# The first stage of a hybrid SSD and retention layer: tokens first in the load queue, and two k-tiles of weights for three token blocks while two blocks arrive

## The chip, the cores and the metric

The kernel runs on one NeuronCore of one Trainium2 chip. The metric is the time of one execution on the device in microseconds. The engines are TensorE (PE, its weight loads PEld), VectorE (DVE), ScalarE (ACT), GpSimd (POOL), and SyncE (SP), which issues nearly all loads.

## What is computed

One layer of a bidirectional mixer for 640 tokens: 128 context tokens (token block 0, with modulation from `c_ctx`) and 512 latent tokens (blocks 1 to 4, with modulation from `c`). The reference, cut to what matters here:

```python
mod = jax.nn.silu(cond) @ w_mod + b_mod              # (1024) @ (1024, 3072)
shift, scale, gate = jnp.split(mod, 3, axis=-1)
h = _rms(x, norm_pre_w) * (1 + scale) + shift        # (tokens, 1024)
u = h @ w_in                                         # then split: z, xbc, dt, q, k, v, g
# SSD scan on xbc and dt, retention on q, k, v, both directions, each gated
out = mix @ w_out
y = x + gate * _rms(out, norm_post_w)
```

`_rms(x, w)` divides each token by the root of its mean square and multiplies by `w`. The first stage of the kernel makes h, all 640 tokens by 1024 channels, and with it the first 512 columns of u (256 columns of v and 256 of g).

## The kernel before, in words

Tokens come in five blocks t = 0..4 of 128 rows, channels in eight k-tiles kt = 0..7 of 128. Every product is made of three matmuls on split operands: a float32 value is a rounded high half and a low half, and hi x hi, hi x lo and lo x hi are added in PSUM.

The first stage is written as a list of steps, START (line 44): a letter and a k-tile or token block. The loop at line 352 issues each step's instructions in that order; a scheduler may let neighbours pass each other on an engine, but each engine then works strictly in its order. The steps:

- M kt (`load_wm`, line 245): SP loads the shift and scale columns of w_mod for k-tile kt, 128 x 2048, 1 MB, into one of three buffers (wm). W kt (`load_w0`, 250): the first 512 columns of w_in for k-tile kt, 256 KB, one of three buffers (raw). L t (`load_x`, 255): token block t, 512 KB, five buffers (x).
- A kt (`mod_a`, 290): modulation of k-tile kt on TensorE, 8 matmuls of 32 x 256 in 16 passes (mod<-wm,silc), and a copy on VectorE (ms). B kt (`mod_b`, 312): two small products that turn the row into columns (mod<-idt,ms), then two VectorE instructions that give shift and scale per channel (ash).
- N t (`norm_x`, 273): square and sum of a token block on ScalarE (hl<-x, L274), the power -0.5 on POOL (rs), and the scaling of its first 128 channels on VectorE. R t (`rest_x`, 337): the scaling of the other 896 channels, on VectorE after h of k-tile 0.
- H kt:ts (`h_tile`, 320): for token blocks ts, transposes on TensorE into PSUM (tr<-idt,x), on ScalarE scale and shift (h<-tr,ash, one instruction for block 0 and one for the others), on VectorE the split into halves (hh, hl).
- S kt (`split0`, 302): ScalarE rounds raw to w0h, VectorE makes w0l. G kt:ts (`gemm0`, 341): for each token block three matmuls of 128 x 512 (acc<-w0h,hh; acc<-w0l,hh; acc<-w0h,hl) into that block's PSUM bank.
- Z n (`warm`, 285): 4n matmuls of 128 x 128 on a tile of zeros, whose results nobody reads. F n: loads of the next stage's weights. C: two tables (cst, rope).

All loads of START stand in one queue of SP, in the order of the steps. When G7 is done, the next stage starts with the product gt (`gemm_tok`) on h of all k-tiles; the rest of the kernel follows an order of slots and does not depend on START.

```python
    for op in START.split():
        k = int(op[1])
        if op[0] == "H":
            h_tile(k, [int(t) for t in op[3:]])
        elif op[0] == "G":
            for t in op[3:]:
                gemm0(k, int(t))
```

Of the kernel before, what the change touches and what calls it, by code (L numbers as in the profile page):

```python
# [25 lines left out]
Z0, XS0, B0, C0, DT0, Q0, K0, V0, G0 = 0, 1024, 2048, 2560, 3072, 3104, 3616, 4128, 5152  # L26
# [15 lines left out]


START = """
M0 Z2 W0 L0 L1 L2 L3 L4 M1 W1 M2 N0 S0 A0 B0 H0:0 G0:0 R0 Z4 N1 H0:1 N2 N3 R1 H0:2 G0:1 H0:3 W2 M3
N4 W4 R2 R3 H0:4 R4 A1 S2 G0:4 W3 G0:3 B1 S1 S3 G0:2 H1:4 A2 W5 H1:0123 M4 B2 M5 H2:012 H2:3 H2:4
G1:01 G1:2 G2:12 G2:3 A3 G1:34 G2:4 B3 H3:0123 S4 G2:0 A4 H3:4 M6 G3:012 B4 H4:0123 H4:4 A5 G3:34 C0
M7 W7 S5 W6 B5 H5:0123 G4:012 A6 G4:34 F2 S6 B6 H5:4 H6:0123 H6:4 G5:012 A7 G5:34 F2 B7 S7 H7:0123
G6:34 G6:012 H7:4 F2 G7:012 G7:34
"""  # L50


# [53 lines left out]
def body(ctx, tc, io):  # L106
# [23 lines left out]
    def tt(out, a, b, op, eng=vec):  # L130
        return eng.tensor_tensor(out=out, in0=a, in1=b, op=op)  # L131
# [50 lines left out]
    def feed(ahead_load=4, ahead_split=2):  # L182
        while state["ld"] < min(len(want), state["use"] + ahead_load):
            pieces[state["ld"]] = load_split(state["ld"])
            state["ld"] += 1
        while state["sp"] < min(state["ld"], state["use"] + ahead_split):
            pieces[state["sp"]][2]()
            state["sp"] += 1
# [84 lines left out]
    def norm_x(t):  # L273
        act.activation(junk, xs_t[t], AF.Square, scale=1.0 / 32, accum_out=ss[:, t:t + 1])  # L274
        tt(rs[:, t:t + 1], ss[:, t:t + 1], mhalf[:, 0:1], ALU.pow, eng=pool)
        scale_x(t, slice(0, P), vec)

    def scale_x(t, q, eng):
        eng.tensor_scalar(xs_t[t][:, q], xs_t[t][:, q], rs[:, t:t + 1], None, op0=ALU.mult)
# [5 lines left out]
    def warm(n):  # L285
        wps = bank("warm")
        for _ in range(4 * n):
            mm(wps[:, 0:P], wz, wz, True, True)
# [31 lines left out]
    def h_tile(kt, ts):  # L320
        ash = ash_t[kt]
        h32 = st_.tile([P, 512], F32, tag="h32", name="h32", bufs=3)[:, 0:len(ts) * P]
        tr = bank("tr")
        for n, t in enumerate(ts):
            pe.transpose(tr[:, n * P:(n + 1) * P], xs_t[t][:, kt * P:(kt + 1) * P], ident)
        for c, u in ((0, [t for t in ts if t == 0]), (1, [t for t in ts if t])):
            if u:
                q = slice((u[0] - ts[0]) * P, (u[-1] + 1 - ts[0]) * P)
                act.activation(h32[:, q], tr[:, q], AF.Identity,
                               bias=ash[:, c:c + 1], scale=ash[:, 2 + c:3 + c])  # L330
        q = slice(ts[0] * P, (ts[-1] + 1) * P)
        vec.tensor_copy(hh[:, kt, q], h32)
        r = tt(hl[:, kt, q], h32, hh[:, kt, q].bitcast(F32), ALU.subtract)
        if kt == 0:
            h_last[ts[0]] = getattr(r, "ins", r)
# [5 lines left out]
    def gemm0(kt, t):  # L341
        wh, wl = w0[kt]
        s = slice(t * P, (t + 1) * P)
        mm(acc[t], hh[:, kt, s], wh, kt == 0, False)
        mm(acc[t], hh[:, kt, s], wl, False, False)
        mm(acc[t], hl[:, kt, s], wh, False, kt == KT - 1)

    acc = [pg.tile([P, 512], F32, tag="g", name="acc0") for _ in range(5)]
    steps = {
        "M": load_wm, "W": load_w0, "L": load_x, "A": mod_a, "S": split0, "B": mod_b, "N": norm_x, "R": rest_x,  # L350
    }
    for op in START.split():
        k = int(op[1])
        if op[0] == "H":
            h_tile(k, [int(t) for t in op[3:]])
        elif op[0] == "G":
            for t in op[3:]:
                gemm0(k, int(t))
        elif op[0] == "Z":
            warm(k)  # L360
        elif op[0] == "F":
            feed(k, 0)
        elif op[0] == "C":
            sp.dma_start(out=cst, in_=io["cst"])
            sp.dma_start(out=rope, in_=io["rope"])
        else:
            steps[op[0]](k)


    R = {}  # L370
# [90 lines left out]
    S = {}  # L461
# [482 lines left out]
    op = tc.alloc_tile_pool(name="op", bufs=1, side="right")  # L944
# [207 lines left out]
```

## Time and profile before

| | |
|---|---|
| median of 3 runs | 607.87 us (607.24 to 608.06) |
| profiled execution | 606.02 us, span 604.0 us, mean granted clock 0.993 |
| TensorE busy | 582.3 us (96% of the span) |
| VectorE / ScalarE / POOL busy | 418.1 (69%) / 337.4 (56%) / 31.3 us (5%) |
| DMA | 87.44 MB, 145 GB/s mean over the span |
| chain of waits that ended last | TensorE 65%, VectorE 13%, ScalarE 9%, DMA 6% |

The span runs from the first to the last instruction; the execution's own time has 2.0 us around it. A busy share is an average over stages with different limits, so the first stage is read from its own stretch. In a timeline row, "xN" is how many instructions were merged, and the bracket is the idle time before the row with what ended it.

### The profile page before, as it was taken

The page shows a single profiled execution, that of the slowest core. Times are in us where ns is not written, and L with a number is a line of the kernel's source. Part 1 is how long each engine was busy: PE and PEld are TensorE (multiplying, and loading weights), DVE is VectorE, ACT ScalarE, POOL GpSimd, SP SyncE. Part 2 cuts the span into 40 slices and gives each one's busy share as a digit, 9 for nine tenths or more (in the row PEclk, how much of TensorE's full clock was granted, in tenths as well). Part 3 has the DMA queues.
Part 4 walks back from the last instruction along what each step waited for, and adds up shares of the span by engine and source line. Part 5 has one row for each costly group of instructions (what it writes and reads, how often), then busy time and mean ns, then how long its engine had stood idle before and what let it go on. Part 6 is the DMA issues. An engine that isn't in the chain of part 4 may idle for free.

```text
span 604.0 us, 10966 instructions
## 1 busy us (share of the span) xinstructions
PE 582.3 (96%) x3833; PEld 521.5 (86%) x3833; DVE 418.1 (69%) x942; ACT 337.4 (56%) x934; POOL 31.3 (5%) x112
## 2 busy tenths in 40 slices
PE   5899998999999999999999999999999999999995
PEld 3577998978999998889999888999999777788895
DVE  3657498855698866668897746798867866743665
ACT  5436255665667764465766646566755857262421
POOL 1000001200000010000011000000110000000010
PEclk9899999999999999999999999999999999999998
DMA  8694231553335633232554223354537777384033
GB/s 348 229 362 161 63 105 48 162 146 109 99 97 159 185 91 86 80 122 70 189 172 112 76 69 105 102 163 131 160 96 223 209 266 221 116 272 120 18 109 135
DMA packets 47638, 87.44 MB, mean 145 GB/s; under 512 B 5792, under 2 KB 18656, under 8 KB 46048
## 3 DMA queue, kind: packets, MB, share of 16 engines
q1 hardware_dynamic: 47296, 86.57, 45.2%
q8 instruction: 30, 0.49, 0.3%
q14 instruction: 24, 0.20, 0.1%
q10 hardware_dynamic: 288, 0.18, 0.1%
HBM read 75.03 MB, written 9.60 MB: 140 GB/s over the span
## 4 chain that ended last, share of the span: by engine, by line
PE 65%; DVE 13%; ACT 9%; DMA 6%; issue 5%; POOL 2%; SPq 0%; POOLq 0%; DVEq 0%; ACTq 0%
PE gw L123 24%; PE gc L123 11%; PE gt L123 9%; PE acc L123 5%; PE go L123 4%; DMA cf<-cumd 3%; PE ss L123 2%; PE mod L123 2%; DVE wlo L131 2%; DVE SC L128 2%; PE sfb L123 1%; PE ry L123 1%; POOL sm L131 1%; DVE yc L128 1%; ACT jk L733 1%
## 5 line engine op out<-in xcount | busy, mean ns | idle before, releaser
L131 DVE TENSOR_TENSOR wlo<-raw,whi 128x512 fp32r<-128x512 f32 (+1 forms) x120 | 82.2, 690 | 49.2 <-ACT whi L174 48.3
L174 ACT CAST whi<-raw 128x512 fp32r<-128x512 f32 (+1 forms) x120 | 73.6, 619 | 76.3 <-PE gw L123 46.1
L123 PE MATMUL gc<-hh,whi 128*128 128x320 f32 x384 | 96.7, 331 | 0.0
L123 PE MATMUL gc<-hl,whi 128*128 128x320 f32 x384 | 88.3, 310 | 0.0
L123 PE MATMUL gc<-hh,wlo 128*128 128x320 f32 x384 | 87.6, 309 | 0.0
L123 PEld LDWEIGHTS gc<-hh,whi 128*128 128x128 f32 x384 | 63.9, 189 | 1.1
L123 PEld LDWEIGHTS gc<-hl,whi 128*128 128x128 f32 x384 | 64.3, 188 | 0.1
L123 PEld LDWEIGHTS gc<-hh,wlo 128*128 128x128 f32 x384 | 64.1, 188 | 0.0
L123 PE MATMUL gw<-whi,hh 128*128 128x512 f32 x120 | 50.6, 421 | 0.8 <-ACT u L484 0.8
L123 PE MATMUL gw<-whi,hl 128*128 128x512 f32 x120 | 47.0, 392 | 0.0
L123 PE MATMUL gw<-wlo,hh 128*128 128x512 f32 x120 | 46.8, 390 | 0.0
L123 PE MATMUL gt<-whi,hh 128*128 128x256 f32 (+1 forms) x160 | 46.3, 289 | 0.0
L123 PE MATMUL gt<-wlo,hh 128*128 128x256 f32 (+1 forms) x160 | 45.7, 286 | 0.0
L123 PE MATMUL gt<-whi,hl 128*128 128x256 f32 (+1 forms) x160 | 45.7, 286 | 0.0
L862 ACT ACTIVATE m<-gu,dt 128x128 f32<-128x128 f32 x80 | 31.3, 391 | 16.5 <-DVE gu L131 14.6
L834 ACT ACTIVATE cf<-cf,dmc 128x128 f32<-128x128 f32 x80 | 26.5, 393 | 18.4 <-DMA cf<-cumd 18.4
L131 DVE TENSOR_TENSOR m<-m,cf 128x512 f32<-128x512 f32 x40 | 27.5, 689 | 8.8 <-ACT cf L863 8.2
L123 PE MATMUL gw<-whi,mrh 128*128 128x512 f32 x80 | 32.3, 404 | 0.0
L123 PE MATMUL gw<-wlo,mrh 128*128 128x512 f32 x80 | 31.2, 391 | 0.0
L123 PEld LDWEIGHTS gt<-whi,hh 128*128 128x128 f32 x160 | 30.5, 190 | 0.7 <-issue 0.5
L863 ACT ACTIVATE cf<-gu,dt 128x128 f32<-128x128 f32 x80 | 31.0, 387 | 0.0
L123 PE MATMUL gw<-whi,mrl 128*128 128x512 f32 x80 | 30.9, 391 | 0.0
(232 smaller groups left out, 1327.8 us busy)
## 6 DMA issues: line engine op xcount, KB each, us to landing
raw<-ws SPq DMA_DIRECT2D x116, 256.0 KB, 2.8
cf<-cumd SPq DMA_DIRECT2D x20, 512.0 KB, 4.2
wm<-wm SPq DMA_DIRECT2D x8, 1024.0 KB, 8.2
mraw<-mixd SPq DMA_DIRECT2D x16, 320.0 KB, 3.4
ef<-ecumd SPq DMA_DIRECT2D x32, 128.0 KB, 3.3
wg<-wg SPq DMA_DIRECT2D x4, 1024.0 KB, 5.9
x<-x SPq DMA_DIRECT2D x5, 512.0 KB, 7.3
mixd<-rmix SPq DMA_DIRECT2D x20, 128.0 KB, 2.7
```

Of the source, the lines that this page charges most:

```text
L123: r = pe.matmul(out, lhsT=a, rhs=b, start=start, stop=stop)
L128: eng.scalar_tensor_tensor(out=out, in0=in0, scalar=s, in1=in1, op0=op0, op1=op1)
L131: return eng.tensor_tensor(out=out, in0=a, in1=b, op=op)
L174: act.copy(hi, raw)
L733: act.activation(jk, yc[:, h], AF.Square, scale=P ** -0.5, accum_out=sm[:, 2 + h:3 + h])
L834: act.activation(cf[:, e, 1, q], cf[:, e, 1, q], AF.Identity, bias=dmc[:, c, h:h + 1])
L862: act.activation(m[:, e, q], gu[:, 0], AF.Copy, scale=dt[:, c, h:h + 1])
L863: act.activation(cf[:, e, 1, q], gu[:, 1], AF.Copy, scale=dt[:, c, 16 + h:17 + h])
```

## The change

The list START is written anew, and the scaling of the first 128 channels becomes a step of its own, Q, which N included before. Tokens stand first in the load queue and are mixed with the weights of k-tiles 0 and 1; k-tile 0 and 1 are multiplied for blocks 0 to 2 before blocks 3 and 4 follow; from then on a line of the list does the modulation of k-tile kt, the products of k-tile kt-2, and the transposes of kt-1 between these. Z18 stands at the start, further Z steps between the first steps; all of Z come to 132 matmuls instead of 24.

```diff
 START = """
-M0 Z2 W0 L0 L1 L2 L3 L4 M1 W1 M2 N0 S0 A0 B0 H0:0 G0:0 R0 Z4 N1 H0:1 N2 N3 R1 H0:2 G0:1 H0:3 W2 M3
-N4 W4 R2 R3 H0:4 R4 A1 S2 G0:4 W3 G0:3 B1 S1 S3 G0:2 H1:4 A2 W5 H1:0123 M4 B2 M5 H2:012 H2:3 H2:4
-G1:01 G1:2 G2:12 G2:3 A3 G1:34 G2:4 B3 H3:0123 S4 G2:0 A4 H3:4 M6 G3:012 B4 H4:0123 H4:4 A5 G3:34 C0
-M7 W7 S5 W6 B5 H5:0123 G4:012 A6 G4:34 F2 S6 B6 H5:4 H6:0123 H6:4 G5:012 A7 G5:34 F2 B7 S7 H7:0123
-G6:34 G6:012 H7:4 F2 G7:012 G7:34
+L0 M0 L1 W0 L2 M1 W1 L3 L4 M2 W2
+Z18 N0 Q0 N1 A0 M3 Z2 B0 H0:0 Q1 S0 W3 Z4 H0:1 N2 G0:0 R0 Z1 G0:1 R1 A1 M4 Q2 H0:2 R2 B1 S1 W4 G0:2 N3 H1:012 Z6 G1:012
+A2 M5 Q3 N4 H0:3 R3 B2 S2 W5 Q4 Z2 G0:3 H0:4 H1:3 H2:012 G0:4 R4 G1:3 H1:4 H2:3 A3 M6 G2:01 G1:4 H2:4 S3 W6 G2:2 B3
+A4 M7 H3:0123 G2:34 H3:4 S4 W7 B4
+A5 G3:01 H4:0123 H4:4 S5 G3:234 B5 C0
+A6 G4:01 H5:0123 H5:4 S6 G4:234 B6 F2
+A7 G5:01 H6:0123 H6:4 S7 G5:234 B7 F2
+G6:01 H7:0123 H7:4 F2 G6:234
+G7:01234
 """
...
     def norm_x(t):
         act.activation(junk, xs_t[t], AF.Square, scale=1.0 / 32, accum_out=ss[:, t:t + 1])
         tt(rs[:, t:t + 1], ss[:, t:t + 1], mhalf[:, 0:1], ALU.pow, eng=pool)
+
+    def first_x(t):
         scale_x(t, slice(0, P), vec)
...
-        k = int(op[1])
+        k = int(op[1:].split(":")[0])
```

How this moves instructions, engine by engine; "acc_120" to "acc_124" are the PSUM banks of token blocks 0 to 4, "x5" is five equal instructions. SP's queue of loads at the start, before:

```order
L247 DMA wm<-wm 128x2048
L252 DMA raw_136<-w 128x512
L258 DMA x<-x 128x1024 x5
L247 DMA wm<-wm 128x2048
L252 DMA raw_155<-w 128x512
L247 DMA wm<-wm 128x2048
```

and now:

```order
L262 DMA x<-x 128x1024
L251 DMA wm<-wm 128x2048
L262 DMA x<-x 128x1024
L256 DMA raw_133<-w 128x512
L262 DMA x<-x 128x1024
L251 DMA wm<-wm 128x2048
L256 DMA raw_140<-w 128x512
L262 DMA x<-x 128x1024 x2
L251 DMA wm<-wm 128x2048
```

The modulation weights of k-tile 0 stand behind one token block, those of k-tile 1 behind three instead of five.

TensorE around the second modulation, before, from the last of the single transposes of k-tile 0 on:

```order
L325 MATMUL tr<-idt,x 128x128 x2
L123 MATMUL acc_124<-w0h,hh 128x512
L123 MATMUL acc_124<-w0l,hh 128x512
L123 MATMUL mod<-wm,silc 32x256 x8
L123 MATMUL acc_124<-w0h,hl 128x512
L123 MATMUL acc_123<-w0h,hh 128x512
L123 MATMUL acc_123<-w0l,hh 128x512
L123 MATMUL acc_123<-w0h,hl 128x512
L123 MATMUL mod<-idt,ms 128x2 x2
L123 MATMUL acc_122<-w0h,hh 128x512
L123 MATMUL acc_122<-w0l,hh 128x512
L123 MATMUL acc_122<-w0h,hl 128x512
```

and now, the nine matmuls of k-tile 1 that end at the third modulation:

```order
L127 MATMUL acc_120<-w0h,hh 128x512
L127 MATMUL acc_120<-w0l,hh 128x512
L127 MATMUL acc_121<-w0h,hh 128x512
L127 MATMUL acc_120<-w0h,hl 128x512
L127 MATMUL acc_121<-w0l,hh 128x512
L127 MATMUL acc_121<-w0h,hl 128x512
L127 MATMUL acc_122<-w0h,hh 128x512
L127 MATMUL acc_122<-w0l,hh 128x512
L127 MATMUL acc_122<-w0h,hl 128x512
L127 MATMUL mod<-wm,silc 32x256 x8
L331 MATMUL tr<-idt,x 128x128
```

Before, all five blocks of k-tile 0 are multiplied before the third modulation and none of k-tile 1; now three blocks of both k-tiles are.

VectorE at the start, before, from the modulation's conditioning on:

```order
L266 TENSOR_SCALAR silc<-thc 128x8x2
L600 TENSOR_SCALAR lamp<-lamp 128x8
L131 TENSOR_TENSOR w0l<-raw_136,w0h 128x512
L297 COPY ms<-mod 128x256
L317 TENSOR_SCALAR ash<-mod,pk 128x2
L318 TENSOR_SCALAR ash<-mod,bs_114,pk 128x2
L279 TENSOR_SCALAR x<-x,rs 128x128 x2
L332 CAST hh<-h_182 128x128
L131 TENSOR_TENSOR hl<-h_182,hh 128x128
L279 TENSOR_SCALAR x<-x,rs 128x896
```

and now:

```order
L303 COPY ms<-mod 128x256
L285 TENSOR_SCALAR x<-x,rs 128x128
L323 TENSOR_SCALAR ash<-mod,pk 128x2
L324 TENSOR_SCALAR ash<-mod,bs_114,pk 128x2
L285 TENSOR_SCALAR x<-x,rs 128x128
L338 CAST hh<-h_257 128x128
L135 TENSOR_TENSOR hl<-h_257,hh 128x128
L285 TENSOR_SCALAR x<-x,rs 128x896
L135 TENSOR_TENSOR w0l<-raw_133,w0h 128x512
```

The low half of k-tile 0's weights, w0l, stood ahead of the modulation's copy; now it stands behind block 0's halves and the rest of block 0. From the first gt on, the order of all engines is the same in both.

## Rows read from the trace of the kernel before

**Rows 1.** Busy time of the engines by stretch of the span: stretch and its length in us, then busy us (and instructions) of PE, PEld, DVE, ACT and POOL, the granted clock of TensorE, the busy share of the DMA engines, and GB/s.

```profile
8.00:24.00 16.00, 12.44 (x67) 7.97 (x60) 8.52 (x27) 7.59 (x15) 3.00 (x5) 0.89 0.89 361
24.00:62.50 38.50, 38.41 (x263) 28.08 (x262) 26.13 (x73) 21.77 (x49) 0.00 (x0) 1.00 0.68 233
```

**Rows 2.** The same view and columns, in slices of 1 us.

```profile
17.00:18.00 1.00, 0.23 (x1) 0.14 (x1) 0.54 (x3) 0.00 (x0) 0.39 (x1) 1.00 0.96 399
18.00:19.00 1.00, 0.14 (x2) 0.04 (x1) 0.97 (x4) 0.46 (x1) 0.00 (x0) 1.00 1.13 436
...
20.00:21.00 1.00, 1.00 (x13) 0.48 (x16) 0.00 (x0) 0.00 (x0) 0.00 (x0) 0.50 0.96 401
...
22.00:23.00 1.00, 1.00 (x4) 0.84 (x5) 0.42 (x1) 0.00 (x0) 0.00 (x0) 0.77 0.01 4
```

**Rows 3.** Timeline of the first stage, matmuls and load issues: start in us, duration in us, engine, line, operation, tiles out<-in, count, and the idle time before it.

```profile
0.72 0.39 SPq L247 DMA_DIRECT2D wm<-wm  x1
1.02 1.03 PE L123 MATMUL warm<-wz 128*128 128x128 bf16 x8 [1.02 <-POOL x L257]
1.63 4.81 SPq L258 DMA_DIRECT2D x<-x  x5
6.88 1.93 PE L123 MATMUL mod<-wm,silc 128*32 128x256 f32 x16 [4.82 <-DVE silc L266]
9.36 1.01 PE L123 MATMUL mod<-idt,ms 128*128 128x2 f32 x4 [0.55 <-DVE ms L297]
11.33 1.91 PE L123 MATMUL warm<-wz 128*128 128x128 bf16 x16
13.11 0.77 PE L123 MATMUL acc<-w0h,hh 128*128 128x512 f32 x1
13.69 0.63 PE L123 MATMUL acc<-w0l,hh 128*128 128x512 f32 x1
14.11 0.63 PE L123 MATMUL acc<-w0h,hl 128*128 128x512 f32 x1
...
23.19 0.50 PE L123 MATMUL mod<-idt,ms 128*128 128x2 f32 x4
24.34 0.27 PE L325 MATMUL tr<-idt,x 128*128 128x128 f32 x1
24.54 1.07 PE L123 MATMUL mod<-wm,silc 128*32 128x256 f32 x16
39.05 3.29 SPq L168 DMA_DIRECT2D raw<-ws  x4
62.11 0.40 PE L123 MATMUL acc<-w0l,hh 128*128 128x512 f32 x1
62.34 0.40 PE L123 MATMUL acc<-w0h,hl 128*128 128x512 f32 x1
62.58 0.29 PE L123 MATMUL gt<-whi,hh 128*128 128x288 f32 x1
```

**Rows 4.** The chain of waits that ended last, in order of time: start in us, us, what.

```profile
15.35 1.15 ACT hl L274 x2
16.57 0.84 POOL rs L131
...
62.74 15.99 PE gt L123 x120
```

**Rows 5.** Load issues of three short stretches (0 to 0.9 us, 1.5 to 1.7, 39.0 to 39.5): tiles out<-in, queue, count, KB, us from issue to landing.

```profile
wm<-wm SPq DMA_DIRECT2D x1, 1024.0 KB, 5.2
x<-x SPq DMA_DIRECT2D x1, 512.0 KB, 6.5
raw<-ws SPq DMA_DIRECT2D x1, 288.0 KB, 8.5
```

**Rows 6.** The stretch view again, columns as in rows 1, for 10 to 20 us.

```profile
10.00:20.00 10.00, 6.99 (x31) 4.90 (x31) 7.03 (x22) 5.91 (x13) 2.46 (x4) 0.95 1.04 423
```

**Rows 7.** Timeline of ScalarE and VectorE in the first stage, columns as in rows 3.

```profile
7.05 0.60 ACT L306 CAST w0h<-raw 128x512 fp32r<-128x512 f32 x1
7.68 0.69 DVE L131 TENSOR_TENSOR w0l<-raw,w0h 128x512 fp32r<-128x512 f32 x1 [0.78 <-ACT w0h L306]
8.88 0.42 DVE L297 COPY ms<-mod 128x256 f32<-128x256 f32 x1 [0.51 <-PE mod L123]
10.41 0.22 DVE L317 TENSOR_SCALAR ash<-mod,pk 128x2 f32<-128x2 f32 x1 [1.10 <-PE mod L123]
10.55 0.27 DVE L318 TENSOR_SCALAR ash<-mod,bs,pk 128x2 f32<-128x2 f32 x1
11.58 0.46 ACT L329 ACTIVATE h<-tr,ash 128x128 f32<-128x128 f32 x1 [0.96 <-PE tr L325]
12.07 0.23 DVE L332 CAST hh<-h 128x128 fp32r<-128x128 f32 x1 [0.51 <-ACT h L329]
12.33 0.29 DVE L131 TENSOR_TENSOR hl<-h,hh 128x128 fp32r<-128x128 f32 x1
12.54 0.68 DVE L279 TENSOR_SCALAR x<-x,rs 128x896 f32<-128x896 f32 x1
...
28.09 1.61 ACT L329 ACTIVATE h<-tr,ash 128x128 f32<-128x128 f32 x4 [0.77 <-PE tr L325]
29.03 0.58 DVE L332 CAST hh<-h 128x384 fp32r<-128x384 f32 x2 [0.46 <-ACT h L329]
```

More of the change, by code (lines that the diff above doesn't have):

```diff
@@ L349, in body @@
     steps = {
-        "M": load_wm, "W": load_w0, "L": load_x, "A": mod_a, "S": split0, "B": mod_b, "N": norm_x, "R": rest_x,
+        "M": load_wm, "W": load_w0, "L": load_x, "A": mod_a, "S": split0, "B": mod_b, "N": norm_x, "Q": first_x, "R": rest_x,
     }
     for op in START.split():
-        k = int(op[1])
+        k = int(op[1:].split(":")[0])
         if op[0] == "H":
```

## The prediction

> **What bounds the kernel now.** I read the table by stages first [rows 1]. From 24.0 to 62.5 us TensorE is busy for 38.41 of 38.50 us at a granted clock of 1.00: there the end is set by how much TensorE work is left, and by nothing else. From 8 to 24 us it is busy for 12.44 of 16.00. The first stage ends at 62.58, where the next product (gt) starts [rows 3]. So the question is not what a wait costs in the middle of the stage, but when the stage has as little work left as before has at 24.34.
>
> The early part loses time twice. First, the clock. One modulation (16 passes) takes 1.93 us at 6.88 and 1.07 at 24.54; products follow each other by 0.42 us (13.69 to 14.11) and later by 0.23 (62.11 to 62.34) [rows 3]: the engine runs at 1.2 GHz at first and at 2.4 later. The clock column gives 1.00 before its first record, so for the first 15 us the durations decide. TensorE is 23% and 14% busy from 17 to 19 us, then the granted clock is 0.50, and it is back within the slice 22 to 23 [rows 2]. Second, the tokens. The chain of waits runs through squares, POOL and scale of the late token blocks (15.35, and 16.57 + 0.84) [rows 4], since at that time nothing but k-tile 0 can be multiplied: k-tile 1's modulation weights stand behind all five blocks in the load queue.
>
> **The loads.** The first load (wm, 1,024 KB), issued at 0.72, lands after 5.2 us [rows 3, 5], at 5.9; the queue moves 423 GB/s [rows 6]. So 0.524 MB of tokens take 1.24 us, 1.049 MB of wm 2.48, 0.262 MB of w0 0.62. In the new order: x0 at 4.7, wm0 7.1, x1 8.4, w0(0) 9.0, x2 10.2, wm1 12.7, w0(1) 13.3, x3 14.6, x4 15.8, wm2 18.3. The same sum for before's x0 gives 7.8, and the rows 1.63 + 6.5 = 8.1 [rows 3, 5]: 0.3 us is its error. Against before, wm0 is 1.2 us later and wm1 is some 3 us earlier.
>
> **To the first product.** The 72 warm matmuls are new. Eight took 1.03 us and sixteen 1.91, so one is 0.11 at the lower clock [rows 3]: from 1.0 they end at 8.9 if the clock stays low, and at half that duration they would end before wm0 is there. The conditioning (silc) is ready at 6.88 [rows 3], its load stands on ScalarE's queue as before. Modulation 0 thus starts between 7.1 and 8.9; I take 7.9, with the clock rising inside the warm matmuls and 1.07 for the modulation: 9.0. The Trainium skill, page TensorE: Matmul & The Clock Gate, section Part 1: The HAM clock gate (the "warmup" mystery), says that the clock is low by default, that activity releases it, and that the moment of the rise shifts from run to run. By that the start would differ between executions by some tenths of a microsecond; no run here shows that yet, and the durations of [rows 3] show one rise.
>
> Then, with durations from [rows 7]: ms 0.42 (9.4), its two transposing products 0.50 [rows 3] (9.9), ash 0.22 + 0.27 (10.4), h 0.46 (10.9), hh 0.23 (11.1). The split of w0 now stands behind h: cast 0.60 (11.4, the first product may start), and its low half on VectorE behind hl 0.29 and the rest of x0 0.68: 11.1 + 0.97 + 0.69 = 12.8. Two products more at 0.23, then block 1's three: 13.9. Before, the first product is at 13.11, and five blocks of k-tile 0 are done at 24.34, where the next transpose starts [rows 3]. POOL's five powers and the squares lie beside this: x0 is there at 4.7, and a square with its sum takes about 1.15 [rows 4].
>
> **k-tile 1 for three blocks.** Modulation 1 (wm1 there at 12.7) stands on TensorE behind block 1: 13.9 to 15.0. ms 0.42 (15.4), two products 0.50 (15.9). VectorE then has, in its order, the low half of w0(1) 0.69 from 15.4, hh and hl of block 2, 0.23 + 0.29, the rest of x2, 0.68, and the two ash, 0.22 + 0.27: 17.8. Behind VectorE's ash wait h of the three blocks, then hh, then the products. h in two instructions: four took 1.61 [rows 7], I take 0.9 (18.7); hh of 384 columns: 384 + 128 took 0.58, less 0.22: 0.36 (19.1). Nine products at 0.23: **21.2**. The warm matmuls of Z6 lie in this wait; should the wait be shorter than they are, 24 x 0.055 = 1.3 us is the most that they could cost.
>
> **What is left from there.** Before, from 24.34: 105 of the 120 products, 35 of the 40 transposes, six modulations with their two products each, done in 62.58 - 24.34 = 38.24 us [rows 3]. Changed, from 21.2: 102 products (-3 x 0.23 = -0.69), 34 transposes (some -0.1), the same six modulations, and eight warm matmuls (+0.44 at half of 0.11). 37.9 us, so the stage ends at 59.1: **3.5 us earlier**. Transposes placed between products cost the same instructions; I cost that at nothing, because VectorE and ScalarE work beside TensorE (26.13 and 21.77 of 38.5 us [rows 1]); if that cover failed, one late h would cost about h + hh, 0.7 us, a time. Blocks 3 and 4 now meet their waits after the cut, as before met them from 24 to 28; either way up to 0.7 us. "Modulation two k-tiles ahead" lets wm 3 to 7 be asked for earlier: a k-tile's load is 2.48 + 0.62 = 3.1 us against fifteen products, a modulation and its transposes, 3.5 + 1.07 + some 1.0 us of TensorE, so loads stay ahead. The weights of the next stage stand behind wm7 in the queue. The first of them landed at 39.05 + 8.5 = 47.6 [rows 3, 5], 15 us before use; they move with wm7, which waits for modulation 4, and keep most of that.
>
> Behind the stage the order of every engine is the same, so I pass the whole gain on. The profiled execution is 606.02 us (span 604.0 and 2.0 around it): 602.5 for it. The median of the runs is 607.87, 1.85 above: 604.4.
>
> **Rivals.**
> - *The clock falls in between.* The changed order multiplies while loads still arrive, and a fall costs what it cost at 19 to 22.5 [rows 2]: about 3.5 us at half rate, 1.75 us of work. One fall: 604.4 + 1.75 = 606.1. Two: 607.9. For it: the waits at 11 to 13 and 16 to 19. Against it: the 52 warm matmuls that stand in just these waits, and that the clock held at 1.00 from 24 to 62.5 with transposes and modulations mixed in. The Trainium skill, page TensorE: Matmul & The Clock Gate, section Loop structure matters more than you think, has the rule behind this: products that wait for a load each time let the clock drop. The trace agrees for 17 to 19 us, at 23% and 14% busy [rows 2].
> - *The clock does not rise before 21 us* (the other side). If the warm matmuls do not raise it, TensorE does all up to the cut at the low rate: 18 products x 0.19 = 3.4, two modulations x 0.86 = 1.7, their products 2 x (1.01 - 0.50) = 1.0, the 52 warm matmuls behind the first 72 x 0.055 = 2.9; about 9 us [rows 3], of which the waits take in a third. 6 us worse than the forecast: 610.4. It decides once low stretches before the cut cost over 3.5 us of TensorE's path, that is over 7 us of low clock. Against it: sixteen warm matmuls and the products around them were followed by products 0.23 apart.
> - *The change does not reach the end.* A later wait (the next weights, VectorE, which runs through squares and state work of the next stage) takes the gain back: 607.9. The chain has 16 us of pure TensorE (gt) right behind the stage [rows 4], which speaks against it.
>
> **How the numbers follow.** Forecast 604.4, chance 0.62; its own range 603.2 to 605.6 (modulation 0 at 7.1 or 8.9: -0.8 to +1.0; waits of blocks 3 and 4: +-0.5 or so). A larger gain, with the warm matmuls shorter and fewer waits, below 603.2: 0.03. One fall of the clock, 606.1: 0.15. Two, 607.9: 0.05. Not passed on: 0.08. Slower: 0.07. A measurement here can tell about 0.2%, 1.2 us, from no change. Faster by more: 0.62 + 0.03 + 0.15 = 0.80; within: 0.05 + 0.08 = 0.13; slower 0.07. The range 603.0 to 607.2 leaves out the two falls, the lost gain and the slow case, and the edge below, some 0.2.
>
> **What would show it.** Right: gt starts near 59.1 us; the modulation at 7 to 9 us takes about 1.07; six blocks of products lie before the third modulation, which starts near 21; no granted clock of 0.50 between 9 and 25. Wrong: a modulation at 1.93 behind the warm matmuls, a slice of 0.50 after 10 us, a first product later than 13, or a TensorE wait of over 1 us behind 25 us; and, for the third rival, gt at 59 with the end where it was.

## The result, and the profile after

The changed kernel takes 603.35 us (median of 5 runs, 602.09 to 603.58) beside 607.87 (median of 5, 607.24 to 610.48): 0.9915 of it, 95% interval 0.9890 to 0.9939. That is 4.5 us by the medians and 5.2 by the ratio; 3.5 were forecast, and 607.87 x 0.9915 = 602.7 lies below the range of 603.0 to 607.2 (the plain median, 603.35, lies just inside it). The direction and the mechanism in the first stage were right, the size was not. Three slow executions in the experiments below took 824, 965 and 2024 us, and no median counts them. The two profiled executions differ by only 2.66 us (606.02 and 603.36; spans 604.0 and 601.4), so the result already holds a riddle: most of the forecast can be checked in the trace and fits, and the runs gain more than the traces show.

The stage by stretches, columns as in [rows 1]:

```profile
8.00:24.00 16.00, 14.10 (x146) 9.86 (x138) 9.12 (x27) 8.75 (x17) 2.58 (x4) 1.00 1.03 417
24.00:62.50 38.50, 38.40 (x260) 29.84 (x260) 26.57 (x79) 22.10 (x52) 0.27 (x6) 1.00 0.65 225
```

TensorE is busy for 14.10 of the 16 us where it was busy for 12.44, at a granted clock of 1.00 instead of 0.89, and the loads move 417 GB/s over the whole stretch where they moved 361 [rows 1] (423 from 10 to 20 us [rows 6]). The 1-us slices that answer to [rows 2], same columns:

```profile
17.00:18.00 1.00, 1.00 (x10) 0.66 (x10) 0.76 (x3) 0.07 (x1) 0.73 (x1) 1.00 0.94 393
18.00:19.00 1.00, 0.69 (x12) 0.51 (x9) 0.20 (x1) 0.83 (x3) 0.00 (x0) 1.00 1.03 399
19.00:20.00 1.00, 0.47 (x2) 0.43 (x3) 0.85 (x2) 1.00 (x3) 0.00 (x0) 1.00 1.00 414
20.00:21.00 1.00, 1.00 (x6) 0.81 (x5) 0.29 (x2) 0.32 (x3) 0.54 (x1) 1.00 1.04 432
...
22.00:23.00 1.00, 1.00 (x18) 0.44 (x11) 0.06 (x1) 0.00 (x0) 0.00 (x0) 1.00 1.09 442
```

TensorE was 23% and 14% busy at 17 and 18 us, and then at 0.50; now it is 100% and 69% busy there and 47% at 19 us, and stays at 1.00. (The clock column also reads 1.00 before its first record, so the durations below have to bear it out.) Its timeline, columns as in [rows 3]:

```profile
1.02 6.72 PE L127 MATMUL warm<-wz 128*128 128x128 bf16 x72 [1.02 <-POOL x L261]
7.75 1.07 PE L127 MATMUL mod<-wm,silc 128*32 128x256 f32 x16
...
11.56 0.48 PE L127 MATMUL acc<-w0h,hh 128*128 128x512 f32 x1
12.85 0.50 PE L127 MATMUL acc<-w0l,hh 128*128 128x512 f32 x1 [0.81 <-DVE w0l L135]
...
14.21 1.07 PE L127 MATMUL mod<-wm,silc 128*32 128x256 f32 x16
...
19.52 0.51 PE L127 MATMUL acc<-w0h,hh 128*128 128x512 f32 x1 [0.84 <-DVE hh L338]
...
21.81 1.07 PE L127 MATMUL mod<-wm,silc 128*32 128x256 f32 x16
...
59.40 0.29 PE L127 MATMUL gt<-whi,hh 128*128 128x288 f32 x1
```

The first modulation takes 1.07 us instead of 1.93; the third starts at 21.81, with six blocks of products done; gt starts at 59.40, 3.18 us earlier than in [rows 3]. Behind 2 us two waits of more than 0.2 us are left, of 0.81 and 0.84. In the chain that ended last (columns as in [rows 4]) one load of tokens and one square (two instructions, x2) lead, through steps of POOL, VectorE and ScalarE that are left out here, into a row of products:

```profile
1.62 7.32 DMA x<-x
...
9.05 1.16 ACT hl L278 x2
...
19.52 2.35 PE acc L127 x9
21.88 1.00 PE mod L127 x16
...
59.56 16.00 PE gt L127 x120
```

### The profile page after: what moved, and what is told of

The parts are those of the page before. It is cut to its first block, busy times and chain, and to the rows that moved or that the text cites. A ratio compares the mean times of both kernels' runs of the same rounds, so it can differ in the third digit from the quotient of the medians.

```text
span 601.4 us, 11185 instructions
## 1 busy us (share of the span) xinstructions
PE 585.7 (97%) x3941; PEld 527.5 (88%) x3941; DVE 417.1 (69%) x944; ACT 338.0 (56%) x935; POOL 31.3 (5%) x112
## 4 chain that ended last, share of the span: by engine, by line
PE 62%; DVE 12%; ACT 9%; DMA 9%; issue 5%; POOL 2%; SPq 0%; DVEq 0%; POOLq 0%; ACTq 0%
PE gw L127 22%; PE gc L127 11%; PE gt L127 9%; PE acc L127 5%; DMA cf<-cumd 5%; PE go L127 4%; DMA mraw<-mixd 2%; PE ss L127 2%; PE mod L127 2%; DVE SC L132 2%; DVE wlo L135 1%; PE sfb L127 1%; DVE m L135 1%; DMA x<-x 1%; POOL sm L135 1%
```

## The experiments

Two theories were set against each other on where the missing 1 to 2 us are. **A**: before's early clock differs from execution to execution, and its profiled execution was a lucky one. **B**: the part behind the stage, with the same instructions in both kernels, varies or has become shorter. "Stage end" is the start of the first gt in a run's profile, "rest" the span less that. A factor with its interval is the ratio of runs to before's runs on the same chip.

### Both kernels again

*Before, unchanged.* 

> The kernel before, unchanged, to see how its executions differ. Known so far: the profiled execution took 606.02 us (stage ends at 62.58, granted clock 0.50 for one stretch of 3.4 us in the first 25 us), the five timed ones 607.24 to 610.48; the changed kernel's profiled one 603.36 beside a median of 603.35. Theory A (the clock): before's first stage has short work and long waits, so how long its TensorE stands at the lower level differs between executions, and the profiled one was a lucky one. Then the mean granted clock of its runs lies at 0.993 or below and the longer runs have the lower clock (0.5 us of time for each us at 0.50, about 0.0008 of the mean clock for 0.5 us), and another profile has the stage's end elsewhere, 61 to 64.5 us, with the stretches at 0.50 in other places. Theory B (elsewhere): the 1.9 us between the profile and the median come from transfers and waits behind the stage; then the stage ends at 62.6 within 0.3 in this profile too, the clock is 0.993 in all runs, and runs differ at one clock. Theory C (chance alone): the new runs centre on 606 rather than 607.9.

Measured: 606.8 us (median of 12; 0.998, 0.9957 to 1.0002), stage end 62.62, rest 542.1. One stretch at 0.50 as in the first profile, no 2 us more in the stage. The median lies between the 606 of chance alone (theory C of the expectation) and 607.9; over all 130 runs of before it is 607.8.

> One more profile of the kernel before, for one of its other executions. Two so far end the stage at 62.58 and 62.62, each with one stretch of 3.4 us at 0.50 from 19.0 or 19.5 us. Before's runs have mean clocks from 0.988 to 0.999: a run at 0.988 or 0.989 has some 7 us more at 0.50 than those two have. By theory A such a profile shows it in the first 30 us, with the stage's end at 64 to 66 us; if it comes at 0.993 to 0.996 again, the stage ends at 62 to 63 again.

Measured: 609.54 us, stage end 63.57, rest 543.9. Slices of 1 us, columns as in [rows 1]:

```profile
17.00:18.00 1.00, 0.18 (x1) 0.18 (x1) 0.53 (x4) 0.00 (x0) 0.44 (x1) 0.78 0.97 401
18.00:19.00 1.00, 0.30 (x1) 0.00 (x0) 1.00 (x3) 0.46 (x1) 0.00 (x0) 0.50 1.10 426
...
21.00:22.00 1.00, 1.00 (x12) 0.20 (x4) 0.00 (x0) 0.00 (x0) 0.00 (x0) 0.50 0.76 293
22.00:23.00 1.00, 1.00 (x6) 0.78 (x3) 0.42 (x1) 0.00 (x0) 0.00 (x0) 0.50 0.02 8
23.00:24.00 1.00, 1.00 (x4) 0.71 (x4) 0.00 (x0) 0.00 (x0) 0.00 (x0) 0.50 0.06 16
24.00:25.00 1.00, 1.00 (x7) 0.96 (x6) 0.27 (x2) 0.00 (x0) 0.00 (x0) 0.81 0.00 0
```

Here the lower level lasts until 24 us, while in [rows 2] it ended within the slice at 22: A exists, and the stage ends 1.0 us later. But 2.5 of the 3.5 us that this run takes more than the first profiled one lie in the rest: B exists too.

> Before again, for the stage's end and the rest in one more execution. So far 62.58 + 541.4, 62.62 + 542.1, 63.57 + 543.9. Theory A alone (the early clock makes all the spread) wants the rest at 541 to 542 and the stage's end at 62 to 66; theory B (transfers behind the stage) the stage at 62.6 and the rest at 541 to 545. By what is known now both vary: 62 to 65 and 541 to 544, with the long waits near 122 and 482 us wherever the rest is over 542.

Measured: 608.54 us, stage end 62.48, rest 544.0.

> As the look before it: before once more, stage end 62 to 65, rest 541 to 544.

Measured: 606.89 us, stage end 61.25 (earlier than expected; no slice at 0.50 between 14 and 25 us), rest 543.6.

*The changed kernel, unchanged.* 

> The changed kernel, unchanged, with more runs. So far before's runs spread from 604.4 to 611.6 us at mean clocks of 0.988 to 0.999, the changed kernel's from 602.1 to 603.6 at 0.996 to 0.999. Theory A (the clock of the first stage varies in before and no longer in the changed kernel): the new runs stay within some 2 us, at 0.996 or above, median 603.3 within 0.5; the stage ends at 59.4 within 0.3. Theory B (the spread comes from transfers behind the stage, which the change leaves alone): the runs spread as before's do, over 5 us and more, and the median is as uncertain.

Measured: 602.76 us (median of 6; 0.9916, 0.9889 to 0.9942), all between 602.0 and 604.0; stage end 59.39, rest 540.6.

> The changed kernel once more: stage end 59.4 within 0.1 if the clock is held in every execution, rest 540.5 to 542. If the rest varies here as much as in before (over 543), then what is behind the stage is chance and gives the change nothing; if it stays below 542, the shorter rest belongs to the change too.

Measured: 602.77 us, stage end 59.25, rest 541.6.

*Before's list and order, with the changed kernel's code* (step N of each token block split into N and Q, always together):

```diff
-M0 Z2 W0 ... N0 S0 A0 B0 ... N1 H0:1 N2 N3 R1 ...
+M0 Z2 W0 ... N0 Q0 S0 A0 B0 ... N1 Q1 H0:1 N2 Q2 N3 Q3 R1 ...
```

> Before's list and before's order of instructions on every engine, written with the changed kernel's code (N and Q apart, and Q always right behind N). It is the control of the code itself: it should be before. Open is the part of the time behind the stage. It took 541.4, 542.1 and 543.9 us of the span in three profiles of before, 542.0 and 540.6 in two of the changed kernel; one wait in it (ScalarE for mraw<-mixd near 482 us) was 0.9, 1.7, 2.2 and 1.4 us in four profiles of kernels written with before's code and 0.3 to 0.7 in five of five looked at with the changed code. If the code itself (where its instructions lie) does that: this kernel shows some 0.5 us there and runs 1 us faster than before, 606.5 to 607. If it is chance, or what the stage ahead leaves to the loads: before's numbers, 607.9 within 1, stage end 62 to 64, rest 541 to 544.

Measured: 608.0 us (median of 12; 1.0008, 0.9983 to 1.0033), stage end 62.81, rest 542.1. The code's form does nothing that these runs can tell. Z18, the held clock and the loads with Z18, below, are written in this form too, and their edits are shown without Q.

With a fourth profile of the changed kernel (its last repeat, at the end of the experiments: 59.71 and 539.9) the split is

| profiles | stage end | rest |
|---|---|---|
| before's order, 6 | 62.58, 62.62, 63.57, 62.48, 61.25, 62.81: mean 62.55 | 541.4, 542.1, 543.9, 544.0, 543.6, 542.1: mean 542.85 |
| changed, 4 | 59.40, 59.39, 59.25, 59.71: mean 59.44 | 542.0, 540.6, 541.6, 539.9: mean 541.0 |

3.1 us of the gain are the stage, and 1.85 the rest: together 5.0, as the runs have it. Before's profiled execution had the shortest rest of its six, the changed kernel's the longest of its four. The rest differs above all in two places. From the matmuls at 119 us of before's first profile to those at 128, its five others take 0.9 to 2.2 us longer, the changed kernel's four 0.1 less to 0.6 longer. There ScalarE waits for cf, a load from DRAM, and behind it TensorE's rz and gw wait for yc and u. Waits in us in total, times, longest, over 118 to 132 us, in before's first profile and in b_look2, and (115 to 129 us) in the changed kernel:

```profile
ACT cf L834 <- DMA cf<-cumd: 1.5, 2, 1.1
PE rz L747 <- DVE yc L128: 0.5, 1, 0.5
```

```profile
ACT cf L834 <- DMA cf<-cumd: 3.6, 2, 2.4
PE rz L747 <- DVE yc L128: 1.3, 1, 1.3
PE gw L123 <- ACT u L484: 1.3, 1, 1.3
```

```profile
ACT cf L840 <- DMA cf<-cumd: 0.9, 2, 0.5
PE rz L753 <- DVE yc L132: 0.9, 1, 0.9
```

ScalarE's wait for cf is 1.5 to 3.6 us in the six and 0.7 to 1.0 in the four; rz alone waits 0.5 to 2.0 and 0.7 to 1.3. The second place is near 480 us: from 416 to 485, before's other five take 0.2 to 1.3 us longer than its first profile, the changed kernel's four 0.7 to 0.8 less. ScalarE waits there for mraw, again from DRAM, and TensorE's sy behind it. The first is b_look's profile (470 to 486 us), the second the changed kernel's (466 to 482), columns as above:

```profile
ACT mrh L1009 <- DMA mraw<-mixd: 3.1, 2, 2.2
PE sy L123 <- DVE m L131: 1.8, 1, 1.8
```

```profile
ACT mrh L1015 <- DMA mraw<-mixd: 1.4, 2, 0.7
```

sy waits in every one of before's six profiles (0.3 to 1.8 us) and in none of the four after, though the instructions there are the same and stand in the same order.

The ten other profiles of this case, the variants below, say how far this goes. The four with before's steps (Z18, clock held, loads, loads with Z18) have rests of 540.9, 544.0, 544.8 and 541.7 us, the six with the changed steps (8 warm matmuls, none, only the 72, old loads, the split first and again) 542.1, 541.8, 540.2, 540.4, 539.9 and 541.0. By steps, ten against ten, the means are 542.8 and 540.9, with some overlap. So the shorter rest goes with the changed list of steps rather than with a stage that ends early or a clock that stays up: the changed steps with the old loads end the stage at 64.63, later than any other, and have 540.4; before's with the clock held have 544.0. Followed matmul by matmul on TensorE, the first place makes 0.9 us of the difference and the second 1.3 by the means of six and four, 0.9 and 1.0 by those of ten and ten. At the second, sy waits in eight of the ten with before's steps (not in the two that have Z18 and nothing else new in the waits) and in none of the other ten. At the first the waits for cf overlap: 0.5 us with before's steps and Z18, 2.3 with the changed steps and 8 warm matmuls. Why the loads land earlier was not found: SP issues them at the same distance from the stage's end (cf 52.7 and 53.0 us behind it).

### The clock alone

*72 warm matmuls instead of 8 at before's start:*

```diff
-M0 Z2 W0 L0
+M0 Z18 W0 L0
```

> Before's list with one edit: 72 warm matmuls at its start instead of 8. Order and loads stay. Theory A says how much of the change is the early clock alone. Were the clock full from 6 us on and never back, modulation 0 and all up to 24 us would go at the double rate and the stage would end near 59.9: 603.4 us in time, the whole gain. But the order keeps its waits for tokens at 17 to 19 us, where TensorE was 23% and 14% busy, so I expect it to fall there again, and the stage to end between 61 and 63: 604.5 to 606.5 us, 1 to 3 below before's median. The rival (the order and the loads bring all, the clock nothing): 607.9, and a stage end of 62.6 or later, since 64 more warm matmuls stand ahead of modulation 0.

Measured: 605.7 us (median of 9; 0.9961, 0.9933 to 0.9989), stage end 61.42. The first modulation takes 1.07 us, yet TensorE is at 0.50 again, twice, from 11.5 and from 18.4 us (means over three us, columns as in [rows 1]):

```profile
11.00:14.00 3.00, 2.85 (x17) 1.92 (x14) 2.22 (x8) 2.71 (x7) 1.27 (x3) 0.59 1.04 425
14.00:17.00 3.00, 1.59 (x5) 0.69 (x4) 2.42 (x9) 1.79 (x5) 1.17 (x2) 0.84 1.02 409
17.00:20.00 3.00, 2.20 (x18) 0.89 (x18) 1.64 (x5) 0.43 (x1) 0.00 (x0) 0.73 1.02 414
```

As expected, the clock falls back. By the factor, an early clock that is not held brings 2.4 of the 5 us in this order.

*The clock held in before's order*, with 76 more warm matmuls in its waits (the expectation says 84, but its own items add up to 76):

```diff
-S0 A0 B0 H0:0 G0:0 ... R1 H0:2 G0:1 H0:3 ... R3 H0:4 R4 A1 S2 G0:4
+S0 A0 Z3 B0 Z2 H0:0 G0:0 ... R1 Z2 H0:2 G0:1 Z6 H0:3 ... R3 Z4 H0:4 R4 A1 S2 Z2 G0:4
```

(on top of Z18). 

> Before's steps and before's load order, with the clock held: 72 warm matmuls at the start, and 84 more placed in just the waits that the run with 72 alone showed on TensorE (12 behind the first modulation, 8 behind its two products, 8 and 24 around the third block's transposes, 16 and 8 behind the fourth's and ahead of the last block's products). The question is how much of the change's gain is the clock, with no help from order or loads. Theory A: the granted clock goes up by 7 us and has no stretch at 0.50 before the last 10 us; the runs have 0.996 or more and lie within 3 us of each other; some warm matmuls lie on the path (up to 1.5 us), so the stage ends at 60.5 to 61.6: 603.9 to 605.1 us, 3 to 4 below before's median of 608. Rival: the order and the loads carry the gain and a held clock is worth little by itself: stage end 62.5 or later, 607 to 609 us.

Measured: 606.6 us (median of 12; 0.9982, 0.9962 to 1.0003), stage end 61.10, rest 544.0. In the stage A is right: no slice below 1.00, and 1.5 us less than before's mean with neither new order nor new loads. The runs neither show nor exclude these 1.5 us: their interval goes from 2.3 us faster to 0.2 slower. The profiled execution loses most of them behind the stage: its rest is 1.1 us above before's mean. At 122 us rz waits 1.9 us, and TensorE runs at 0.50 behind it (columns as in [rows 1]):

```profile
122.00:123.00 1.00, 1.00 (x4) 0.78 (x5) 0.77 (x2) 0.72 (x3) 0.00 (x0) 0.57 0.88 264
123.00:124.00 1.00, 1.00 (x4) 0.81 (x3) 0.25 (x1) 1.00 (x5) 0.00 (x0) 0.50 0.77 266
124.00:125.00 1.00, 1.00 (x3) 0.78 (x3) 0.44 (x1) 1.00 (x4) 0.00 (x0) 0.50 0.06 23
125.00:126.00 1.00, 1.00 (x5) 0.75 (x4) 0.45 (x1) 1.00 (x4) 0.00 (x0) 0.72 0.35 99
```

So a late load in the rest costs its wait and at times the clock as well. Before's stage with the clock held is 1.7 us worse than the changed one; that part is order and loads, less whatever the 76 warm matmuls themselves cost on TensorE's path, which was not measured.

### The changed kernel with less

*8 warm matmuls at the start instead of 72:*

```diff
-Z18 N0 Q0 N1 A0
+Z2 N0 Q0 N1 A0
```

> The changed kernel with 8 warm matmuls at the start instead of 72; everything else as changed. If the opening warm matmuls carry the clock (theory A in its strict form), TensorE stands at the lower level until 10 to 13 us: modulation 0 takes 1.9 us instead of 1.07, the first products 0.42 each; what of that is not taken in by waits is 0.6 to 1.2 us: stage end 60.0 to 60.6, 604.0 to 604.6 us. If the order alone brings the gain: 603.4, stage end 59.4. If without them the clock also falls later: stage end 62 and 606.

Measured: 605.5 us (median of 12; 0.9957, 0.9932 to 0.9982), stage end 61.58, rest 542.1. The clock is full only from 15.8 us; k-tile 1's products start at 21.69 instead of 19.52. This is 2.2 us of stage, nearly twice the strict form's upper end (1.2), and no stretch at 0.50 follows.

*No warm matmuls:*

```diff
-Z18 N0 Q0 N1 A0 M3 Z2 B0 H0:0 Q1 S0 W3 Z4 H0:1 N2 G0:0 R0 Z1 G0:1 ... Z6 G1:012 ... Z2 G0:3
+N0 Q0 N1 A0 M3 B0 H0:0 Q1 S0 W3 H0:1 N2 G0:0 R0 G0:1 ... G1:012 ... G0:3
```

> The changed kernel without any warm matmul (132 fewer); order and loads as changed. My sum: the clock rises with the products, somewhere from 10 to 16 us, and what is done at half rate before that costs, less the waits that take it in and less the warm matmuls that are gone (eight of them and part of others stood on the path, some 0.5 us): stage end 58.8 to 60.8, 602.8 to 604.8 us. So by the theory that the order (work for TensorE from the first token on) is what keeps the clock, nearly all of the gain stays: about 603.8. By the theory that the warm matmuls keep it: the clock stays low up to 20 us or falls once more, stage end 62 or later, 606 or more.

Measured: 604.4 us (median of 12; 0.9937, 0.9915 to 0.9959), but between 603.0 and 607.3; the profile is of one of its longest (606.95: stage end 63.13, at 0.50 until 25.4 us). The median fits "the order keeps most", the profile fits "the clock falls". Six of the twelve runs lie below 604 us at mean clocks of 0.996 to 0.999, so both seem to happen, in different executions; none of these six was profiled.

*Only the 72 at the start:*

```diff
-... Z2 B0 ... Z4 H0:1 ... Z1 G0:1 ... Z6 G1:012 ... Z2 G0:3
+... B0 ... H0:1 ... G0:1 ... G1:012 ... G0:3
```

> The changed kernel with the 72 opening warm matmuls and without the 60 later ones. If the opening ones are enough, TensorE has 60 matmuls less, of which those of Z6 and Z4 lay in waits: stage end 58.9 to 59.5, 602.9 to 603.4 us, in a spread as small as the changed kernel's. If the later ones are what holds the clock in the waits between the first products (without any warm matmul it was full from 18.55, back at 0.50 at 21.97 and full from 25.38 us), the clock falls once in some executions between 9 and 22 us: stage end up to 60.8, runs between 603 and 605, median 604, mean clock 0.993 in the longer ones.

Measured: 605.9 us (median of 12; 0.9966, 0.9946 to 0.9986), mean clocks 0.985 to 0.995, stage end 62.20. A miss of about 2 us for both expectations: its TensorE rose by 7 us and went back to 0.50 twice (columns as in [rows 1]):

```profile
14.00:17.00 3.00, 3.00 (x21) 1.08 (x20) 0.51 (x3) 0.62 (x1) 0.09 (x1) 0.50 1.04 425
17.00:20.00 3.00, 2.22 (x11) 1.35 (x9) 2.45 (x8) 2.09 (x5) 0.59 (x1) 0.96 1.02 406
20.00:23.00 3.00, 2.24 (x5) 1.82 (x6) 1.20 (x3) 1.86 (x4) 0.54 (x1) 0.61 1.02 415
```

The warm matmuls between the products, which seemed to lie in waits and to cost or bring little, hold the clock that the first 72 raise. Without them the first 72 bring nothing over none at all (605.9 beside 604.4).

### The loads

*The changed kernel with before's load order:*

```diff
-L0 M0 L1 W0 L2 M1 W1 L3 L4 M2 W2
+M0 W0 L0 L1 L2 L3 L4 M1 W1 M2 W2
```

> The changed kernel with the load queue in before's order (wm and w0 of k-tile 0, five token blocks, then k-tiles 1 and 2); steps and warm matmuls as changed. If tokens-first carries the gain, wm of k-tile 1 lands some 3 us later than in the changed kernel (about 15.7 instead of 12.7), and with it the second modulation and the products of k-tile 1 that stand ahead of blocks 3 and 4: stage end 61 to 61.5, 604.9 to 605.4 us, with the clock up. If the order of the steps and the clock carry it: 603.4, stage end 59.4. If the longer wait lets the clock fall as well: stage end 62 to 63 and 606.

Measured: 608.8 us (median of 12; 1.0006, 0.9986 to 1.0026), stage end 64.63: the whole gain is lost. TensorE, columns as in [rows 3]:

```profile
14.24 0.40 PE L127 MATMUL acc<-w0h,hl 128*128 128x512 f32 x1
17.14 1.93 PE L127 MATMUL mod<-wm,silc 128*32 128x256 f32 x16 [2.51 <-DMA wm<-wm]
```

The wait for k-tile 1's modulation weights lets the clock fall, and the second modulation itself runs at the lower rate. The last of the three expectations was nearest, and still 1.6 us of stage short.

*Before with the new load order, with and without Z18:*

```diff
-M0 Z2 W0 L0 L1 L2 L3 L4 M1 W1 M2
+L0 M0 Z2 L1 W0 L2 M1 W1 L3 L4 M2     (Z18 in the other)
```

> Before with the new load order at the start alone (tokens first, k-tile 1's weights ahead of blocks 3 and 4); steps and warm matmuls as before. With 72 warm matmuls in addition this gave 607.4, the clock back at 0.50 from 18.05 to 24.88 us behind a wait of 3.9 us for the fourth block. So by theory A the loads alone bring nothing either: the steps still multiply k-tile 0 for all five blocks, now with later tokens, and the clock rises at 10 to 13 us and falls at 17 to 19: stage end 61.5 to 63, 605 to 607 us, median within 2 us of before's. By the theory that loads are the gain and the warm matmuls only stood in their way: 603.5 to 604.

> Before's steps with the two other parts of the change: the new load order at the start and 72 warm matmuls. What is missing of the change is the order of the steps (two k-tiles for three blocks, modulation two k-tiles ahead, transposes between products). With Z18 alone before's steps ended the stage at 61.4, with the clock back at 0.50 from 11.5 to 15 and from 18.4 to 21.8 us. If the load order is what counts, tokens no longer hold TensorE at 17 to 19 us, the clock stays and the stage ends near 60: 603.6. If the steps count: their waits stay, the clock falls once or twice, stage end 61.4 to 63, 605 to 606.5 us.

Measured: 606.5 us (median of 12; 0.9985, 0.9962 to 1.0007) and 607.4 (11; 0.9984, 0.9963 to 1.0006), stage ends 61.94 and 64.05. Both intervals include no change. The list still multiplies k-tile 0 for five blocks, whose last ones now come later. With Z18 (columns as in [rows 3]):

```profile
14.35 0.30 PE L327 MATMUL tr<-idt,x 128*128 128x128 f32 x1 [0.50 <-PE acc L123]
18.58 0.47 PE L327 MATMUL tr<-idt,x 128*128 128x128 f32 x1 [3.94 <-DVE x L281]
...
20.27 1.94 PE L123 MATMUL mod<-wm,silc 128*32 128x256 f32 x16
```

Neither the loads alone nor the steps with the old loads bring a gain that these runs can tell: the new loads feed k-tile 1, and the new steps use it.

### A further step

*The changed kernel with the split of k-tile 0's weights first:*

```diff
-B0 H0:0 Q1 S0 W3
+B0 S0 H0:0 Q1 W3
```

> The changed kernel with one step moved: the split of k-tile 0's weights (S0) ahead of block 0's transposes, so that ScalarE's cast and VectorE's low half come before h, its halves and the rest of block 0. In the changed kernel the second product of block 0 waits 0.81 us for that low half (12.85), and the second modulation stands behind these products at 14.21. By the reading that TensorE's path runs through this wait: it shrinks to some 0.4, the second modulation starts near 13.7, the stage ends at 58.9 and the time is 0.5 us less: 602.3 to 602.8. By the reading that the later wait (0.84 at 19.52, for hh of three blocks) is set by the tokens alone: the second modulation starts earlier, the wait at 19.5 grows by the same, and the stage ends at 59.4.

Measured: 601.6 us (median of 6; 0.9905, 0.9873 to 0.9937), stage end 59.80, and not 58.9. The 0.81 us wait is gone and another stands in its place (columns as in [rows 3]):

```profile
13.20 0.39 PE L127 MATMUL acc<-w0h,hl 128*128 128x512 f32 x1
14.62 1.07 PE L127 MATMUL mod<-wm,silc 128*32 128x256 f32 x16 [1.03 <-DMA wm<-wm]
```

The reading that fits is that the load of wm stands right behind the wait that was taken away. When it lands differs between executions: in the last repeat of the changed kernel the second modulation waits 0.46 us for wm and starts at 14.50, in the first three it starts at 14.07 to 14.21 without this wait. Both kernels once more, on one chip:

> The changed kernel with S0 ahead of block 0's transposes, once more, now beside the changed kernel on one chip. Its first runs had a median of 601.58 us, but its profile ended the stage at 59.80, later than the changed kernel's 59.40: the wait for the low half is gone, and the second modulation then waits 1.03 us for its weights (wm, 14.62). So the 1.2 us between the medians can't come from the stage. By the reading that the two ran on different chips and differ by chance: this run's median lies within 0.6 us of the changed kernel's of the same call, about 602.5. By the reading that the earlier split does shorten something behind the stage: 601.5 beside 602.8.

> The changed kernel again, for the comparison and for one more split at the stage's end: 59.25 to 59.4 and a rest of 540.5 to 542, median 602.8, and runs within 2 us of each other, if it does what its three profiles so far show.

Measured: 602.3 us (8 runs, 601.2 to 603.9; stage end 59.40) and 602.7 (7 runs, 601.6 to 603.9; 59.71, rest 539.9). No difference that these runs can tell. In the first of these two profiles wm is there in time and the second modulation starts at 13.62, 0.59 us earlier than in the changed kernel, and still the products of k-tile 1 start at 19.52 as there (columns as in [rows 3]):

```profile
13.62 1.07 PE L127 MATMUL mod<-wm,silc 128*32 128x256 f32 x16
...
15.20 0.62 ACT L312 CAST w0h<-raw 128x512 fp32r<-128x512 f32 x1 [2.20 <-DMA raw<-w]
...
19.52 0.50 PE L127 MATMUL acc<-w0h,hh 128*128 128x512 f32 x1 [0.84 <-DVE hh L338]
```

ScalarE stands at the cast of k-tile 1's weights, 2.20 us, until their load has landed, and h of block 2 and the later squares stand behind it. So two waits of TensorE are left in the changed stage, and a load lies close behind each.

## Why the prediction was right and where it was wrong

- **The bound** held: from 24 us on TensorE is busy for 38.40 of 38.50 us (before: 38.41), and what is left at the third modulation sets the end. 59.40 - 21.81 = 37.6 us were left, 37.9 forecast.
- **To the first product:** modulation 0 at 7.75 (forecast 7.9) at 1.07, first product 11.56 (11.4), its low half 12.85 (12.8), modulation 1 at 14.21 (13.9). One figure of the loads is off without entering the sum: by the forecast's own rates wm of k-tile 1 comes 2.5 us earlier than before, not "some 3". The forecast cited the Trainium skill, page TensorE: Matmul & The Clock Gate, section Part 1: The HAM clock gate (the "warmup" mystery), for a rise that shifts between runs. The traces agree: the same 72 matmuls took 6.72, 6.70, 6.36 and 5.67 us in four executions of the changed kernel, and modulation 0, which waits for its load as well, moved only from 7.54 to 7.76; in the two where the 72 took least, it waited for the load.
- **k-tile 1 for three blocks:** products at 19.52 (19.1), done by 21.81 (21.2). h took 0.91 us (0.9), hh 0.36 (0.36), as rows of ScalarE and VectorE have it:

```profile
18.16 0.91 ACT L335 ACTIVATE h<-tr,ash 128x128 f32<-128x128 f32 x2 [1.09 <-PE tr L331]
19.11 0.36 DVE L338 CAST hh<-h 128x384 fp32r<-128x384 f32 x1 [0.91 <-ACT h L335]
```

- **The stage's gain**, 3.5 us forecast, is 3.18 between the two profiles and 3.1 between the means of six and four. This sum was right to 0.4 us.
- **The step that failed** is the end of the sum: "Behind the stage the order of every engine is the same, so I pass the whole gain on", with "The median of the runs is 607.87, 1.85 above: 604.4". The two amount to 607.87 - 3.5: the change of the rest was put at nothing, because the order there is the same, and before's distance between profile and median was carried over to the changed kernel. The runs show a rest that is 1.85 us shorter by the means of six and four profiles, 1.9 by those of ten and ten. I had priced the rival that later waits take gain back, not that they give some; a larger gain had a chance of 0.03, for shorter waits inside the stage, which is not where it came from.
- **Why the two profiles hid it.** Before's profiled execution has the shortest rest of its six, 1.45 us under their mean, and lies low among the timed runs: 15 of 130 lie at or below 606.02, and their median is 607.8. The changed kernel's has the longest rest of its four, 1.0 us over their mean, and lies 0.6 above the median of its 19 runs (602.8). So the distance of 1.85 us was before's own. (That it equals the shortening of the rest is chance.) That 602.5, the forecast for the profiled execution, lies only 0.3 below the median of the 19 is luck too: it holds before's shortest rest.
- **What makes the spread** is shown in part. By the mean granted clock, before's 130 runs have medians of 610.2 us at up to 0.990 (28 runs), 608.0 at 0.991 to 0.993 (40) and 606.8 at 0.994 or more (62), and all 19 runs of the changed kernel are at 0.996 or more: so theory A would have it. But the mean clock also counts the lower level behind the last products, which begins at 599.3 us in before's first profile and at 603.2 in that of its repeat (0.996, with its stretch at 0.50 in the stage), and no run at 0.990 or less was profiled. That the longest runs lose their time in the stage is therefore not shown. Runs of before at the high clock are still 4.0 us above the changed kernel's, more than the stage's 3.1: theory B, the waits near 122 and 480 us. Twenty profiles support the size of the shorter rest and its two places; the cause of the earlier landings stays open.
- **The rivals.** The clock does not fall between the products, and the warm matmuls there have a part in it: with those alone left out it fell twice (605.9 us). The other-side rival, no rise before 21 us, did not come; of its size is only what before's load order does to the changed list: a late load and the fallen clock together cost 5.2 us of stage (64.63). The third, a gain that is taken back behind the stage, came the other way round. In most of the experiments the clock fell behind a wait: at 17.14 us with the old loads (2.51 us of waiting), at 18.58 with the new loads and Z18 (3.94), at 122 with the clock held (1.9). The Trainium skill, page TensorE: Matmul & The Clock Gate, section Loop structure matters more than you think, has the rule that products which wait for loads let the clock drop. The traces agree at these three places, and not everywhere: behind waits of 2.0 to 2.1 us near 122 us it stayed up in three profiles.

## What to carry to other kernels

A profile is one execution: before it is used as the base of a sum, compare it with the spread of the timed runs, and don't carry its distance from their median over to a kernel that changes what makes the spread. An early clock is worth what the following waits leave of it: in the changed order the fillers that hold it bring 3 us, while in before's order holding it brought no more than raising it (606.6 and 605.7 us). Here order and loads without fillers brought 3.7 us, every other part or combination from nothing to 2.6, and all three 5. Instructions that a change does not touch can still take another time behind it, so a gain in one stage is not passed on one to one. Where a stage starts on loads, put the load order and the order of work into one list and change both, since either alone only moves the wait.

## What the hardware showed that I had not expected

- Of two kernels that differ in 60 matmuls on zeros only, the one without them is 3 us slower (605.9 against 602.8), though they are, by an estimate from the 0.11 us of one at the lower clock and half of it at the higher, 3.3 to 6.6 us of work.
- Waits of 1.9 and 2.2 us amid dense work, at 120 us, were followed by some 3 us at 0.50 (in the profile with the clock held and in the one with the new loads alone), waits of 2.0, 2.0 and 2.1 in the same place by none (before's repeat, b_look, and the changed steps with 8 warm matmuls).
- The same instructions, from the first gt on, take 539.9 to 544.0 us of the span in the ten profiles of before's order and the changed kernel, whose granted clock is 1.00 there until the last 10 us. Waits for loads of data that the kernel itself wrote to DRAM are the visible part of it (ScalarE for cf, 0.7 to 3.6 us in one place).
